# A hybrid decoder layer on one core: the first tokens' stage in an order written by hand, and the rope remainder product on 128 rows

## The chip, the core and the metric

The kernel runs on one core of one Trainium2 chip. A core has five engines that run their own instruction streams beside each other: TensorE (PE in the profile) multiplies matrices, VectorE (DVE), ScalarE (ACT) and GpSimd (POOL) work elementwise, and SyncE (SP) issues most transfers. Transfers run on 16 DMA engines. The metric is the device time of one execution in microseconds (us); the median of several runs is compared.

## The reference

One decoder layer on 512 tokens of width 1024, float32. A normalized input goes through one wide projection `w_in`; a gated linear recurrence (8 heads) and a latent attention (8 heads, causal) work on its columns; both are gated, projected and merged. The parts that the change touches are the first normalization and the scores of the attention:

```python
def rms_norm(x, g):
    y = xf * lax.rsqrt(jnp.mean(xf * xf, axis=-1, keepdims=True) + EPS)
    return (y * g.astype(jnp.float32)).astype(x.dtype)
...
h = rms_norm(x, norm_g[l])
proj = h @ w_in[l]
...
s = (jnp.einsum('bqhd,bkhd->bhqk', qn, k_nope)
     + jnp.einsum('bqhr,bkr->bhqk', qp, k_pe)).astype(jnp.float32) * scale
```

The rope part (`qp`, `k_pe`) has 64 numbers per head, the other part 128.

## The kernel before

**Precision.** A factor is held as two tiles of a shorter float type: a high part (a cast, on ScalarE) and a remainder (the factor minus its high part, on VectorE). A product of two such factors is three products on TensorE, high x high, high x low and low x high (`mm3`, lines 84 to 86). `load_w` fetches 512 KB of a weight into one of three buffers (`w_raw`), casts it (line 105) and subtracts (line 106); `split` does the same for a result in PSUM (lines 144, 145).

**First tokens' stage** (lines 168 to 227). x has four tiles of 128 tokens (t = 0 to 3). Twenty products on zeros (line 179) keep TensorE at work until x is there. x, the identity, the first projection's weights in two halves (`c_first`) and some small parameters are issued by SyncE; the norm weight `ng` is spread by a transfer over 128 partitions (line 190, 512 KB). For each tile: squares with a sum (ScalarE, line 213 or 216), the scale (for tile 0 on VectorE by an integer first guess and three Newton steps, lines 157 to 165; for the others on GpSimd by a power, lines 149 and 150), x times scale times `ng` (line 220, `xn`), eight transposes (line 225), and the split into `hT` (high part and remainder). The first projection, 256 columns from `COL_C`, is written behind that (`proj_tok`, line 271) and makes 24 products per tile of tokens; the next one of 256 columns follows.

**What sets the order.** The program is written without waits; a scheduler orders each engine's stream by a simulated time line, and an engine runs its stream strictly in that order. Transfers carry eight counters in turn (`DMAHW0` to `DMAHW7` in the orders below), and a transfer waits for the last one that used its counter. A weight buffer is free again when line 106 has read it.

**Scores** (`mla_scores`, lines 527 to 551). For a head, four blocks i of 128 queries against 128(i + 1) keys: three products of 128 rows over the part without rope (line 538, `mm3`, `kn` and `qn`), and two for rope. `qp[h % 2]` holds, in 128 rows, the high part of the rope query of this head in its own 64 rows and the remainder in the other 64; `kpe` holds the rope key twice, one copy per half, as high part `kpe[0]` and remainder `kpe[1]`. So one product on 128 rows with `kpe[0]` (line 539) gives high x high plus low x high, and one on the own 64 rows with `kpe[1]` gives high x low. That one is first in odd blocks (line 537) and last in even ones (line 541).

Of the kernel before, what the change touches and what calls it, by code (L numbers as in the profile page):

```python
# [40 lines left out]
def hybrid_layer(ctx: ExitStack, tc: tile.TileContext, a):  # L41
# [110 lines left out]
    def rsqrt_sum(rs, mul, add):  # L152


        v, y, c = [st.tile([P, 2], F32, f"rsq{i}") for i in range(3)]
        ts = nc.vector.tensor_scalar
        ts(v[:, 0:1], rs[:, 0:1], mul, add, op0=ALU.mult, op1=ALU.add)
        ts(v[:, 0:1], rs[:, 1:2], mul, v[:, 0:1], op0=ALU.mult, op1=ALU.add)
        ts(y[:, 0:1].bitcast(I32), v[:, 0:1].bitcast(I32), 1, None, op0=ALU.logical_shift_right)
        ts(y[:, 0:1].bitcast(I32), y[:, 0:1].bitcast(I32), -1.0, float(0x5F3759DF), op0=ALU.mult, op1=ALU.add)  # L160
        ts(v[:, 1:2], v[:, 0:1], -0.5, None, op0=ALU.mult)
        for i in range(3):
            ts(c[:, 0:1], y[:, 0:1], y[:, 0:1], v[:, 1:2], op0=ALU.mult, op1=ALU.mult)
            out = rs if i == 2 else y
            ts(out[:, 0:1], c[:, 0:1], 1.5, y[:, 0:1], op0=ALU.add, op1=ALU.mult)
# [41 lines left out]
    for t in range(NT):
        hs = [slice(n * 512, n * 512 + 512) for n in range(2)]
        sq = st.tile([P, D], F32, "sq", bufs=2)
        rs = st.tile([P, 2], F32, "rs", bufs=2)  # L210
        if t == 0:
            for n in range(2):
                nc.scalar.activation(sq[:, hs[n]], x_sb[t][:, hs[n]], AF.Square, accum_out=rs[:, n : n + 1])
            rsqrt_sum(rs, 1.0 / D, EPS)
        else:
            nc.scalar.activation(sq[:], x_sb[t][:], AF.Square, accum_out=rs[:, 0:1])
            power(rs[:, 0:1], rs[:, 0:1], 1.0 / D, EPS, neg_half[:, 0:1])
        xn = st.tile([P, D], F32, "xn", bufs=2)
        for n in range(2):
            nc.vector.scalar_tensor_tensor(xn[:, hs[n]], x_sb[t][:, hs[n]], rs[:, 0:1], ng[:, hs[n]], op0=ALU.mult, op1=ALU.mult)  # L220
# [528 lines left out]
```

## Time and profile before

| | |
|---|---|
| median of three runs | 653.09 us (653.09 to 654.28) |
| the profiled execution, in all | 653.86 us |
| its span, first to last instruction | 652.1 us |
| mean granted TensorE clock | 0.995 |
| bytes read from and written to memory | 55.53 MB, 2.10 MB |

The time in all is taken around the span. Rows of a time line give start and duration in us, engine and line, the operation, the written tile <- the tiles read, shape and count, and in brackets how long the engine idled before and what ended that. PE is a product, PEld the load of its stationary factor, ACTq and SPq the issue of a transfer. Products overlap, so the distance of two starts says what one costs. A wait row says who waited for whom, the total, how often, and the longest.

### The profile page before, as it was taken

The page shows a single profiled execution, that of the slowest core. Times are in us where ns is not written, and L with a number is a line of the kernel's source. Part 1 is how long each engine was busy: PE and PEld are TensorE (multiplying, and loading weights), DVE is VectorE, ACT ScalarE, POOL GpSimd, SP SyncE. Part 2 cuts the span into 40 slices and gives each one's busy share as a digit, 9 for nine tenths or more (in the row PEclk, how much of TensorE's full clock was granted, in tenths as well). Part 3 has the DMA queues.
Part 4 walks back from the last instruction along what each step waited for, and adds up shares of the span by engine and source line. Part 5 has one row for each costly group of instructions (what it writes and reads, how often), then busy time and mean ns, then how long its engine had stood idle before and what let it go on. Part 6 is the DMA issues. An engine that isn't in the chain of part 4 may idle for free.

```text
span 652.1 us, 9054 instructions
## 1 busy us (share of the span) xinstructions
PE 640.3 (98%) x3537; PEld 541.1 (83%) x3537; DVE 351.4 (54%) x546; ACT 239.1 (37%) x451; POOL 112.6 (17%) x211
## 2 busy tenths in 40 slices
PE   7999999999999999999999999999999999999995
PEld 3998988988998898888788888888888888888884
DVE  5725973784585397456665857745322342434244
ACT  6444333232333224254354545534222222323223
POOL 1105311320331232221213131000000010111011
PEclk9999999999999999999999999999999999999998
DMA  8343241233133014302323242133333323324403
GB/s 279 121 130 98 65 135 61 65 99 95 34 98 97 22 45 130 102 21 76 90 53 93 64 112 70 51 97 94 99 88 91 98 81 100 98 94 153 170 13 116
DMA packets 62023, 60.32 MB, mean 92 GB/s; under 512 B 5814, under 2 KB 57308, under 8 KB 61980
## 3 DMA queue, kind: packets, MB, share of 16 engines
q1 hardware_dynamic: 59628, 55.28, 28.5%
q10 hardware_dynamic: 2128, 3.67, 1.9%
q0 software_dynamic: 224, 0.79, 0.4%
q8 instruction: 28, 0.46, 0.3%
q14 instruction: 15, 0.12, 0.1%
HBM read 55.53 MB, written 2.10 MB: 88 GB/s over the span
## 4 chain that ended last, share of the span: by engine, by line
PE 97%; DMA 1%; DVE 1%; issue 0%; ACT 0%; SPq 0%; POOLq 0%; POOL 0%
PE mm_ps L86 26%; PE mm_ps L84 26%; PE mm_ps L85 26%; PE ax_ps L84 3%; PE ax_ps L85 2%; PE ax_ps L86 2%; PE ax_ps L562 1%; PE ax_ps L394 1%; PE ax_ps L413 1%; DMA w_raw<-w_in 1%; PE ax_ps L539 1%; PE ax_ps L415 1%; PE ax_ps L382 1%; PE ax_ps L541 1%; PE ax_ps L402 1%; PE ax_ps L537 1%
## 5 line engine op out<-in xcount | busy, mean ns | idle before, releaser
L106 DVE TENSOR_TENSOR w_lo<-w_raw,w_hi 128x1024 fp32r<-128x1024 f32 (+3 forms) x94 | 111.2, 1185 | 119.6 <-ACT w_hi L105 115.6
L105 ACT CAST w_hi<-w_raw 128x1024 fp32r<-128x1024 f32 (+3 forms) x94 | 92.0, 979 | 174.4 <-PE mm_ps L85 114.1
L84 PE MATMUL mm_ps<-hT,w_hi 128*128 128x512 f32 x384 | 151.4, 394 | 0.0
L86 PE MATMUL mm_ps<-hT,w_lo 128*128 128x512 f32 x384 | 150.4, 392 | 0.0
L85 PE MATMUL mm_ps<-hT,w_hi 128*128 128x512 f32 x384 | 149.9, 390 | 0.0
L86 PEld LDWEIGHTS mm_ps<-hT,w_lo 128*128 128x128 f32 x384 | 72.1, 188 | 14.9
L85 PEld LDWEIGHTS mm_ps<-hT,w_hi 128*128 128x128 f32 x384 | 72.2, 188 | 14.2
L84 PEld LDWEIGHTS mm_ps<-hT,w_hi 128*128 128x128 f32 x384 | 72.2, 188 | 14.2
L86 PE MATMUL mm_ps<-w_hi,hT 128*128 128x256 f32 (+1 forms) x224 | 63.6, 285 | 0.3 <-DVE hT L145 0.3
L84 PE MATMUL mm_ps<-w_hi,hT 128*128 128x256 f32 (+1 forms) x224 | 63.4, 283 | 0.0
L85 PE MATMUL mm_ps<-w_lo,hT 128*128 128x256 f32 (+1 forms) x224 | 63.3, 283 | 0.0
L86 PEld LDWEIGHTS mm_ps<-w_hi,hT 128*128 128x128 f32 x224 | 43.2, 193 | 0.8 <-DVE hT L145 0.7
L84 PEld LDWEIGHTS mm_ps<-w_hi,hT 128*128 128x128 f32 x224 | 43.3, 193 | 0.4 <-ACT hT L144 0.3
L85 PEld LDWEIGHTS mm_ps<-w_lo,hT 128*128 128x128 f32 x224 | 43.2, 193 | 0.2
L652 POOL TENSOR_TENSOR ma<-ma,z 128x512 f32<-128x512 f32 x8 | 11.8, 1478 | 163.9 <-DVE z L651 163.9
L549 POOL TENSOR_SCALAR p<-p,sm 128x128 f32<-128x128 f32 (+3 forms) x32 | 18.9, 597 | 116.1 <-DVE sm L548 89.7
L339 DVE RECIPROCAL tf<-pr 128x512 f32<-128x512 f32 x8 | 26.8, 3349 | 0.2
L547 ACT ACTIVATE p<-ax_ps,sm 128x128 f32<-128x128 f32 (+3 forms) x32 | 16.8, 528 | 25.3 <-DVE sm L546 20.8
L84 PE MATMUL mm_ps<-ya,w_hi 128*128 128x512 f32 x64 | 25.4, 396 | 0.0
L84 PE MATMUL mm_ps<-yb,w_hi 128*128 128x512 f32 x64 | 25.3, 396 | 0.0
L85 PE MATMUL mm_ps<-yb,w_hi 128*128 128x512 f32 x64 | 25.3, 396 | 0.0
L85 PE MATMUL mm_ps<-ya,w_hi 128*128 128x512 f32 x64 | 25.3, 396 | 0.0
(212 smaller groups left out, 1119.3 us busy)
## 6 DMA issues: line engine op xcount, KB each, us to landing
w_raw<-w_in SPq DMA_DIRECT2D x60, 512.0 KB, 3.8
w_raw<-w_proj_a SPq DMA_DIRECT2D x8, 512.0 KB, 3.4
w_raw<-w_proj_b SPq DMA_DIRECT2D x8, 512.0 KB, 3.4
wo_raw<-w_out SPq DMA_DIRECT2D x8, 512.0 KB, 3.3
w_raw<-w_ukv SPq DMA_DIRECT2D x16, 128.0 KB, 2.5
xr<-x SPq DMA_DIRECT2D x4, 512.0 KB, 7.3
x<-x SPq DMA_DIRECT2D x3, 512.0 KB, 8.0
w_raw<-w_uq SPq DMA_DIRECT2D x8, 192.0 KB, 2.6
```

The lines of the kernel that those rows point to most:

```text
L84: nc.tensor.matmul(ps, lh[lsl], rh[rsl], start=start, stop=False)
L85: nc.tensor.matmul(ps, lh[lsl], rl[rsl], start=False, stop=False)
L86: nc.tensor.matmul(ps, ll[lsl], rh[rsl], start=False, stop=stop)
L105: nc.scalar.copy(hi[:, :o], raw[:, :o])
L106: (lo_eng or nc.vector).tensor_tensor(lo[:, :o], raw[:, :o], hi[:, :o].bitcast(F32), op=ALU.subtract)
L339: nc.vector.reciprocal(rp[:], pr[:])
L382: nc.tensor.matmul(sps[:, sl], kt_[:, sl], v_sb[:, i, (h % 2) * P : (h % 2) * P + P], start=True, stop=True)
L394: nc.tensor.matmul(aps[:, b], ki[:, b], qi[:, b], start=True, stop=True)
L402: nc.tensor.matmul(aps[0:64, i * P + 64 : i * P + P], k64[:, b], q64[:, b], start=True, stop=True)
L547: nc.scalar.activation(p[:, :n], sps[:, :n], AF.Exp, scale=SCALE, bias=sm[:, 1:2], accum_out=sm[:, 2:3])
L549: nc.gpsimd.tensor_scalar(p[:, :n], p[:, :n], sm[:, 3:4], 0.5, op0=ALU.mult, op1=ALU.mult)
L652: nc.gpsimd.tensor_tensor(ma[:, j], ma[:, j], g[:], op=ALU.add)
```

## The change

It has two parts.

In the scores, the remainder product takes all 128 rows of `qp` and `kpe[1]` and always stands last. It then also holds the product of the two remainders, which was left out before. Both halves of `kpe[1]` were filled before too.

The first tokens' stage is written out for TensorE, ScalarE and VectorE in one block whose order the scheduler keeps among its own instructions (it may put others between). The norm weight comes as one row of 4 KB and is spread over the partitions by two products with a row of ones, into PSUM, where line 225 reads it. Tile 0's scale is a square root on ScalarE, a reciprocal and one Newton step. There are eight products on zeros in place of twenty. The first projection's weights are cast and split in pieces of 512 columns, the last piece's subtraction on GpSimd. Each tile's products with one kind of factor stand in groups of four. `ident` is issued by ScalarE, the rope table `ktab` by SyncE right ahead of the second projection's weights.

```diff
-    def rsqrt_sum(rs, mul, add):
...
-    nc.scalar.activation(warm[:], neg_half[:], AF.Tanh)
-    idle = ax_tile()
-    for i in range(N_IDLE):
-        nc.tensor.matmul(idle[:], zero[:, :P], zero[:], start=True, stop=True)
...
-    nc.scalar.dma_start(ng[:], a["norm_g"][0].partition_broadcast(P))
-    nc.sync.dma_start(ident[:], a["c_ident"])
-    c_first = [load_w(w_c0[:, 0:4, :])]
+    nc.scalar.dma_start(ng_row[:], a["norm_g"])
+    nc.scalar.dma_start(ident[:], a["c_ident"])
+    load_c(0)
     load_x(1)
-    c_first.append(load_w(w_c0[:, 4:8, :]))
+    load_c(1)
     load_x(2)
     load_x(3)
...
     nc.sync.dma_start(maskf[:], a["c_masks"])
+    nc.sync.dma_start(ktab[:], a["c_ktab"])
...
+    def c_split(kh, i, eng):
+
+        hi, lo = c_hl[kh]
+        nc.scalar.copy(hi[:, half[i]], c_raw[kh][:, half[i]])
+        eng.tensor_tensor(lo[:, half[i]], c_raw[kh][:, half[i]], hi[:, half[i]].bitcast(F32), op=ALU.subtract)
...
+    FIN = 1
+    with tc.manual_schedule(engines={mybir.EngineType.PE, mybir.EngineType.Activation, mybir.EngineType.DVE}):
+        nc.vector.memset(zero[:], 0.0)
+        nc.vector.memset(ones[:], 1.0)
+        nc.scalar.activation(warm[:], eps[:], AF.Sqrt)
+        idle_mm(5)
+        for n in range(2):
+            nc.tensor.matmul(ng[n][:], ones[:], ng_row[:, half[n]], start=True, stop=True)
+        idle_mm(3)
...
+        for n in range(2):
+            nc.scalar.activation(sq[:, half[n]], x_sb[0][:, half[n]], AF.Square, accum_out=rs[:, n : n + 1])
+        nc.vector.tensor_scalar(v[:], rs[:, 0:1], 1.0 / D, EPS, op0=ALU.mult, op1=ALU.add)
+        nc.scalar.activation(y[:], rs[:, 1:2], AF.Sqrt, scale=1.0 / D, bias=v[:])
+        nc.vector.tensor_scalar(e[:], rs[:, 1:2], 1.0 / D, v[:], op0=ALU.mult, op1=ALU.add)
+        nc.vector.tensor_scalar(e[:], e[:], -0.5, None, op0=ALU.mult)
+        nc.vector.reciprocal(y[:], y[:])
+        nc.vector.tensor_scalar(v[:], y[:], y[:], e[:], op0=ALU.mult, op1=ALU.mult)
+        nc.vector.tensor_scalar(rs[:, 0:1], v[:], 1.5, y[:], op0=ALU.add, op1=ALU.mult)
+        scaled(0)
+        c_split(0, 0, nc.vector)
+        lo0 = turned(0, 0)
+        lo0()
+        c_split(0, 1, nc.vector)
+        lo1 = turned(0, 1)
+        c_product(0, 0, 0)
+        c_product(0, 0, 1, (0, 1))
+        c_product(0, 0, 2)
+        c_product(0, 0, 1, (2, 3))
+        lo1()
+        squares(1)
+        c_split(1, 0, nc.vector)
+        c_split(1, 1, nc.gpsimd)
+        squares(2)
+        c_product(0, 1, 0)
+        c_product(0, 1, 2)
+        c_product(0, 1, 1)
+        scaled(1)
+        lo = [turned(1, 0), turned(1, 1)]
+        for t in range(1, NT):
+            if t + 2 < NT:
+                squares(t + 2)
+            for kh in range(2):
+                lo[kh]()
+            if t + 1 < NT:
+                scaled(t + 1)
+            for kind in (0, 1, 2):
+                c_product(t, 0, kind)
+            if t + 1 < NT:
+                nxt = [turned(t + 1, 0), turned(t + 1, 1)]
+            for kind in (0, 2, 1):
+                c_product(t, 1, kind)
+            lo = nxt
...
-        r = slice((h % 2) * 64, (h % 2) * 64 + 64)
...
-            if i % 2:
-                nc.tensor.matmul(sps[:, :n], qh[r, bl], kpe[1][r, :n], start=True, stop=False)
-            mm3(sps[:, :n], qn, kn, (slice(None), bl), (slice(None), slice(0, n)), i % 2 == 0, False)
-            nc.tensor.matmul(sps[:, :n], qh[:, bl], kpe[0][:, :n], start=False, stop=i % 2 == 1)
-            if i % 2 == 0:
-                nc.tensor.matmul(sps[:, :n], qh[r, bl], kpe[1][r, :n], start=False, stop=True)
+            mm3(sps[:, :n], qn, kn, (slice(None), bl), (slice(None), slice(0, n)), True, False)
+            for x in range(2):
+                nc.tensor.matmul(sps[:, :n], qh[:, bl], kpe[x][:, :n], start=False, stop=x == 1)
```

In the new block `scaled(t)` makes `xn`, `turned(t, k4)` transposes four of its columns' blocks and casts them (its result, called later, is the remainder's subtraction), `squares(t)` gives a tile's scale, and `c_product(t, kh, kind)` does four products of tile t with one half kh of the weight; kind 0 is high x high, 1 high x low, 2 low x high.

How the streams move, at the places that matter. First TensorE in the scores of head 0, blocks 0 and 1, before (`kpe_281` is the high part of the rope key, `kpe_282` its remainder):

```order
L84 MATMUL ax_ps<-kn_2616,qn_2605 128x128
L85 MATMUL ax_ps<-kn_2617,qn_2605 128x128
L86 MATMUL ax_ps<-kn_2616,qn_2606 128x128
L539 MATMUL ax_ps<-kpe_281,qp_2580 128x128
L541 MATMUL ax_ps<-kpe_282,qp_2580 128x128
L537 MATMUL ax_ps<-kpe_282,qp_2580 128x256
L84 MATMUL ax_ps<-kn_2616,qn_2605 128x256
L85 MATMUL ax_ps<-kn_2617,qn_2605 128x256
L86 MATMUL ax_ps<-kn_2616,qn_2606 128x256
L539 MATMUL ax_ps<-kpe_281,qp_2580 128x256
```

The same place after (`kpe_87` high part, `kpe_88` remainder):

```order
L82 MATMUL ax_ps<-kn_2615,qn_2604 128x128
L83 MATMUL ax_ps<-kn_2616,qn_2604 128x128
L84 MATMUL ax_ps<-kn_2615,qn_2605 128x128
L604 MATMUL ax_ps<-kpe_87,qp_2579 128x128
L604 MATMUL ax_ps<-kpe_88,qp_2579 128x128
L82 MATMUL ax_ps<-kn_2615,qn_2604 128x256
L83 MATMUL ax_ps<-kn_2616,qn_2604 128x256
L84 MATMUL ax_ps<-kn_2615,qn_2605 128x256
L604 MATMUL ax_ps<-kpe_87,qp_2579 128x256
L604 MATMUL ax_ps<-kpe_88,qp_2579 128x256
```

The count of products is the same; lines 541 and 537, on 64 rows and side by side across two blocks, have become the second of each pair of line 604, on 128 rows.

Second, ScalarE from the first weight cast to the casts of the second projection's weights, before. In brackets is what a row waits for; the waits of line 105 are for the weight's transfer:

```order
L105 CAST w_hi<-w_raw 128x1024 [waits DMAHW4_49]
L216 ACTIVATE sq,rs<-x 128x1024 [waits DMAHW5_49]
L105 CAST w_hi<-w_raw 128x1024 [waits DMAHW6_49]
L144 CAST hT_148<-ax_ps 128x4x128 [waits PE_49]
L216 ACTIVATE sq,rs<-x 128x1024 [waits DMAHW7_49,DVE_49,Activation_49]
L144 CAST hT_148<-ax_ps 128x4x128 [waits PE_49]
L216 ACTIVATE sq,rs<-x 128x1024 [waits DVE_49,DMAHW0_49,Activation_49,Pool_49]
L144 CAST hT_148<-ax_ps 128x4x128 [waits PE_49] x2
L105 CAST w_hi<-w_raw 128x1024 [waits DMAHW7_49]
L105 CAST w_hi<-w_raw 128x1024 [waits DMAHW0_49]
L144 CAST hT_148<-ax_ps 128x4x128 [waits PE_49] x4
```

And after, from the first weight cast on (line 215 casts the first projection's weights, line 103 the second's, line 235 the transposes):

```order
L215 CAST w_hi<-w_raw 128x512 [waits DMAHW4_49]
L235 CAST hT_112<-ax_ps 128x4x128 [waits PE_49]
L215 CAST w_hi<-w_raw 128x512
L235 CAST hT_112<-ax_ps 128x4x128 [waits PE_49]
L220 ACTIVATE sq,rs<-x 128x1024 [waits DMAHW5_49]
L215 CAST w_hi<-w_raw 128x512 [waits DMAHW6_49]
L215 CAST w_hi<-w_raw 128x512
L220 ACTIVATE sq,rs<-x 128x1024 [waits DMAHW7_49,DVE_49,Activation_49]
L103 CAST w_hi<-w_raw 128x1024 [waits DMAHW0_49]
L103 CAST w_hi<-w_raw 128x1024 [waits DMAHW1_49]
L235 CAST hT_112<-ax_ps 128x4x128 [waits PE_49] x2
```

Before, four casts of transposes (tiles 0 and 1) stand ahead of the two casts of the second projection's weights; after, two (tile 0) do, and tile 1's come behind them.

Third, SyncE's issues after x's third tile, after the change (line 179 is x's last tile, line 198 the rope table, line 100 the second projection's weights):

```order
L179 DMA x<-x 128x1024 [waits DMAHW0_49]
L192 DMA rows<-lb_logits 16x128 [waits DMAHW1_49]
L193 DMA rows<-b_gate 16x128 [waits DMAHW2_49]
L194 DMA rows<-hg_norm_g 1x128 [waits DMAHW3_49]
L195 DMA rows<-q_a_g 3x128 [waits DMAHW4_49]
L196 DMA rows<-kv_a_g 2x128 [waits DMAHW5_49]
L197 DMA maskf<-c_masks 128x256 [waits DMAHW6_49]
L198 DMA ktab<-c_ktab 128x512 [waits DMAHW7_49]
L100 DMA w_raw<-w_in 128x4x256 [waits DMAHW0_49]
L100 DMA w_raw<-w_in 128x4x256 [waits DMAHW1_49,DVE_49]
```

`DMAHW0` is x's last tile here, so the first of these weights is issued when x has landed whole. Before, the masks stood right ahead of the weights, the rope table was issued by GpSimd, and the first weight waited for `DMAHW7`, x's third tile.

More of the change, by code (lines that the diff above doesn't have):

```diff
@@ L12 @@
 U8 = mybir.dt.uint8
-I32 = mybir.dt.int32
 BF16 = mybir.dt.bfloat16
@@ L35 @@
 N_MM = 3
-N_IDLE = 20
 WCH = 1024
@@ L150, in power @@
         nc.gpsimd.tensor_tensor(out, out, expo, op=ALU.pow)
-    def rsqrt_sum(rs, mul, add):
[L155 to L165, printed above, removed]
+    cT = [cpool.tile([P, 5, S], F32R, f"cT{i}") for i in range(2)]
+    kpe = [cpool.tile([P, S], F32R, f"kpe{i}") for i in range(2)]
+    cw = Pool("cwork", "right")
+    ktab = cw.tile([P, NT, 2, NR], F32, "ktab")
+    c_sb = cw.tile([P, NT, 704], F32, "c_sb")
+    rows = cw.tile([38, P], F32, "rows")
+    maskf = cw.tile([P, 2, P], F32, "maskf")
     st = Pool("start", "right")
@@ new lines, in hybrid_layer, with idle_mm @@
+    nc.sync.dma_start(ktab[:], a["c_ktab"])
+    half = [slice(n * 512, n * 512 + 512) for n in range(2)]
+    rss = [st.tile([P, 2], F32, "rs", bufs=2) for _ in range(NT)]
+    xns = [st.tile([P, D], F32, "xn", bufs=2) for _ in range(NT)]
+    ng = [ax_tile() for _ in range(2)]
+    idle = ax_tile()
+    c_ps = [mm_tile() for _ in range(2)]
+    def idle_mm(n):
+        for _ in range(n):
+            nc.tensor.matmul(idle[:], zero[:, :P], zero[:], start=True, stop=True)
+    def c_split(kh, i, eng):
+        hi, lo = c_hl[kh]
+        nc.scalar.copy(hi[:, half[i]], c_raw[kh][:, half[i]])
+        eng.tensor_tensor(lo[:, half[i]], c_raw[kh][:, half[i]], hi[:, half[i]].bitcast(F32), op=ALU.subtract)
@@ new lines, in squares, with scaled, turned @@
+    def squares(t):
+        sq = st.tile([P, D], F32, "sq", bufs=2)
+        nc.scalar.activation(sq[:], x_sb[t][:], AF.Square, accum_out=rss[t][:, 0:1])
+        power(rss[t][:, 0:1], rss[t][:, 0:1], 1.0 / D, EPS, neg_half[:, 0:1])
+    def scaled(t):
+        for n in range(2):
+            nc.vector.scalar_tensor_tensor(xns[t][:, half[n]], x_sb[t][:, half[n]], rss[t][:, 0:1], ng[n][:],
+                                           op0=ALU.mult, op1=ALU.mult)
+    def turned(t, k4):
+        ps = ax_tile()
+        for k in range(4):
+            kk = 4 * k4 + k
+            nc.tensor.transpose(ps[:, k * P : k * P + P], xns[t][:, kk * P : kk * P + P], ident[:])
+        sl = (slice(None), slice(4 * k4, 4 * k4 + 4), slice(t * P, t * P + P))
+        nc.scalar.copy(hT[0][sl], ps[:].rearrange("p (k t) -> p k t", k=4))
+        return lambda: nc.vector.tensor_tensor(hT[1][sl], ps[:].rearrange("p (k t) -> p k t", k=4),
+                                               hT[0][sl].bitcast(F32), op=ALU.subtract)
@@ L230, in hybrid_layer @@
+    st.close()
     par = const.tile([P, 38], F32, name="par")
@@ L260, in hybrid_layer @@
     nc.vector.tensor_scalar(c2[:], lb[:], 0.5, 0.5, op0=ALU.mult, op1=ALU.add)
-    st.close()
-    cT = [cpool.tile([P, 5, S], F32R, f"cT{i}") for i in range(2)]
-    kpe = [cpool.tile([P, S], F32R, f"kpe{i}") for i in range(2)]
-    cw = Pool("cwork", "right")
-    ktab = cw.tile([P, NT, 2, NR], F32, "ktab")
-    nc.gpsimd.dma_start(ktab[:], a["c_ktab"])
-    c_sb = cw.tile([P, NT, 704], F32, "c_sb")
     for c0, w in ((0, 256), (256, 256), (512, 192)):
-        for t2, ps in enumerate(proj_tok(w_in, COL_C + c0, w, hT, None if c0 else c_first)):
+        for t2, ps in enumerate(proj_tok(w_in, COL_C + c0, w, hT) if c0 else c_ps):
             nc.scalar.copy(c_sb[:, 2 * t2 : 2 * t2 + 2, c0 : c0 + w],
```

50 lines of the change are left out of this document (22 added, 28 removed).

## The prediction

> **What bounds the kernel now.** I read the page first (busy shares and the chain that ended last), then who TensorE waited for, then the rows of the two places that the diff touches. The first lines are the page's busy row and chain; the third answers which wait of TensorE is the longest.
>
> ```profile
> PE 640.3 (98%) x3537; PEld 541.1 (83%) x3537; DVE 351.4 (54%) x546; ACT 239.1 (37%) x451; POOL 112.6 (17%) x211
> ...
> PE 97%; DMA 1%; DVE 1%; issue 0%; ACT 0%; SPq 0%; POOLq 0%; POOL 0%
> ...
> PE ax_ps L225 <- DVE xn L220: 3.3, 1, 3.3
> ```
>
> TensorE (PE) is the bound: 97% of the chain is its own work, and its only long wait is 3.3 us for the first normalized tile. So time is to be had in two ways: TensorE's real work starts earlier, or its products follow each other faster. The diff tries one of each. I count a product by the distance from its start to the next start, since busy times overlap.
>
> **The scores (rope remainder on 128 rows).** These are TensorE's products in order of time, with start, duration, line, tiles and shape: a 64-row product standing alone, then the first and the last pair of them.
>
> ```profile
> 321.53 0.34 PE L85 MATMUL ax_ps<-kn,qn 128*128 128x384 f32 x1
> 321.70 0.33 PE L86 MATMUL ax_ps<-kn,qn 128*128 128x384 f32 x1
> 321.96 0.49 PE L537 MATMUL ax_ps<-kpe,qp 64*128 64x512 f32 x1
> 322.39 0.50 PE L84 MATMUL ax_ps<-kn,qn 128*128 128x512 f32 x1
> 322.72 0.39 PE L85 MATMUL ax_ps<-kn,qn 128*128 128x512 f32 x1
> 322.95 0.40 PE L86 MATMUL ax_ps<-kn,qn 128*128 128x512 f32 x1
> ...
> 275.52 0.27 PE L86 MATMUL ax_ps<-kn,qn 128*128 128x128 f32 x1
> 275.63 0.27 PE L539 MATMUL ax_ps<-kpe,qp 128*128 128x128 f32 x1
> 275.83 0.32 PE L541 MATMUL ax_ps<-kpe,qp 64*128 64x128 f32 x1
> 276.00 0.33 PE L537 MATMUL ax_ps<-kpe,qp 64*128 64x256 f32 x1
> 276.25 0.39 PE L84 MATMUL ax_ps<-kn,qn 128*128 128x256 f32 x1
> 276.48 0.28 PE L85 MATMUL ax_ps<-kn,qn 128*128 128x256 f32 x1
> 276.60 0.28 PE L86 MATMUL ax_ps<-kn,qn 128*128 128x256 f32 x1
> ...
> 415.52 0.34 PE L539 MATMUL ax_ps<-kpe,qp 128*128 128x384 f32 x1
> 415.78 0.44 PE L541 MATMUL ax_ps<-kpe,qp 64*128 64x384 f32 x1
> 416.06 0.39 PE L537 MATMUL ax_ps<-kpe,qp 64*128 64x512 f32 x1
> 416.39 0.50 PE L84 MATMUL ax_ps<-kn,qn 128*128 128x512 f32 x1
> 416.73 0.40 PE L85 MATMUL ax_ps<-kn,qn 128*128 128x512 f32 x1
> 416.96 0.40 PE L86 MATMUL ax_ps<-kn,qn 128*128 128x512 f32 x1
> ```
>
> Among products of 128 rows a 384-wide one takes 0.17 (321.53 to 321.70), a 512-wide one 0.23 (322.72 to 322.95), a 256-wide one 0.12 (276.48 to 276.60), a 128-wide one 0.11 (275.52 to 275.63). Around the lone 64-row product, 321.70 to 322.72 is 1.02 for one 384-wide and two 512-wide: 0.17 + 0.23 + 0.23 = 0.63, so 0.39 too much. The first pair: 275.63 to 276.48 is 0.85 against 0.11 + 0.11 + 0.12 + 0.12 = 0.46, 0.39 too much. The last pair: 1.21 against 0.17 + 0.17 + 0.23 + 0.23 = 0.80, 0.41 too much. The excess is paid once per change of row count there and back, whether one or two products stand between. The 32 products of lines 537 and 541 form 24 such groups (16 alone, 8 pairs) in the rows from 275.8 to 416.7; read in the same way they exceed by 0.29 to 0.43 each, 8.8 us in sum. After the change these 32 products have the shape of line 539, which shows no excess between its neighbours, and none are added. So the edit takes up to **8.8 us** off the bounding engine. What could eat some of it is late input, since each head's softmax runs through VectorE, ScalarE and GpSimd between its scores and its transposes, and weights must be cast and split in time. No TensorE wait shows in this stretch, so I take 8.5, with 7.0 to 9.0 as bounds.
>
> The Trainium skill's "TensorE: Matmul & The Clock Gate", section "Packing small matmuls — row/col tiling", says that a weight load overlaps a running product only where the row groups differ; by that, 128 rows after 128 rows would not overlap, and widening would buy nothing. The rows disagree: 256-wide products follow each other every 0.12 us here, and the load between them alone has 0.19:
>
> ```profile
> L84 PEld LDWEIGHTS mm_ps<-w_hi,hT 128*128 128x128 f32 x224 | 43.3, 193 | 0.4 <-ACT hT L144 0.3
> ```
>
> **The first tokens' stage.** Before, in rows of TensorE, ScalarE and VectorE:
>
> ```profile
> 11.78 1.32 PE L225 MATMUL ax_ps<-ident,xn 128*128 128x128 f32 x8 [3.35 <-DVE xn L220]
> ...
> 17.12 0.28 PE L84 MATMUL mm_ps<-w_hi,hT 128*128 128x256 f32 x1
> 17.24 0.28 PE L85 MATMUL mm_ps<-w_lo,hT 128*128 128x256 f32 x1
> ...
> 9.75 1.06 ACT L216 ACTIVATE sq<-x 128x1024 f32<-128x1024 f32 x1 [0.19 <-DMA x<-x]
> ...
> 11.07 1.05 ACT L105 CAST w_hi<-w_raw 128x1024 fp32r<-128x1024 f32 x1 [0.18 <-DMA w_raw<-w_in]
> ...
> 15.53 1.07 ACT L144 CAST hT<-ax_ps 128x512 fp32r<-128x512 f32 x2
> ...
> 18.65 1.05 ACT L105 CAST w_hi<-w_raw 128x1024 fp32r<-128x1024 f32 x1 [1.10 <-DMA w_raw<-w_in]
> ...
> 13.63 1.22 DVE L106 TENSOR_TENSOR w_lo<-w_raw,w_hi 128x1024 fp32r<-128x1024 f32 x1
> 14.77 0.68 DVE L145 TENSOR_TENSOR hT<-ax_ps,hT 128x512 fp32r<-128x512 f32 x1
> ...
> 18.16 1.40 DVE L220 SCALAR_TENSOR_TENSOR xn<-x,rs,ng 128x512 f32<-128x512 f32 x2
> ```
>
> By 17.12 TensorE has started 16 transposes (0.11 each) and 9 products (0.12): 2.8 us of work. From there it runs without a gap, so it stands where a TensorE would that began at 17.1 - 2.8 = 14.3 and never paused. The same number is needed for the change.
>
> Tile 0 gets faster: the 512 KB of the spread norm weight no longer travel beside x, the subtraction of 1.2 us no longer stands ahead of its scale, and three Newton steps become one. But the order of ScalarE shows what then decides: both casts of the *second* projection's weights stand ahead of the casts of tile 1's transposes, and they wait for their transfers. Call W the landing of the second of these (18.6 before, where ScalarE idles 1.10 for it). Then: its cast ends at W + 1.05, tile 1's first cast at W + 1.65 (first products of tile 1), the second at W + 2.15. VectorE's subtraction for that weight, also queued ahead, ends at W + 2.3, tile 1's two remainders at W + 2.9 and W + 3.5, tile 2 scaled (1.40) at W + 4.9, its last transposes issued at W + 5.45 and 12 products later W + 6.85. By then 48 products and 24 transposes are done, 8.35 us, so the equivalent start is W - 1.5. Against 14.3 that is **W - 15.8**.
>
> Rows for W (SyncE's issues of the two transfers, and the page's row on how long such a one takes):
>
> ```profile
> 12.38 0.40 SPq L102 DMA_DIRECT2D w_raw<-w_in  x1
> 13.78 0.38 SPq L102 DMA_DIRECT2D w_raw<-w_in  x1
> ...
> w_raw<-w_in SPq DMA_DIRECT2D x60, 512.0 KB, 3.8
> ```
>
> The second was issued at 13.78 and landed by 18.65: 4.9. After the change the first waits for x's last tile and the second is issued some 0.4 behind it. In the rows above, x and weights land in steps of 1.3 us per 512 KB (9.75, 11.07), which puts x's last tile at 13.7 before. Without the norm weight it comes at least one step earlier (12.4), and at most three, as the slow start beside that transfer goes too (9.8). I take two (11.1), and 4.5 for the transfer, nearer to the 4.9 because two run together again: W = 11.1 + 0.4 + 4.5 = 16.0; from the ends, 9.8 + 0.4 + 3.8 = 14.0 and 12.4 + 0.4 + 4.9 = 17.7. So the stage comes to +0.2 us, between -1.8 and +1.9: **what tile 0 gains is spent waiting ahead of tile 1.**
>
> All else in the stage is covered by that wait. Tile 0's first transposes stood at 11.78; without the subtraction (1.22) and with x one step earlier (1.3) they come by 9.3 at the latest. Then follow 16 transposes and 24 products, 4.6 us, and some 2 us of waits for ScalarE, which does a Square (1.06) and a cast (1.05) between: tile 1's transposes end by 15.9, ahead of W + 1.65 = 17.65. That hides the square root, the weight-spreading products, GpSimd's half subtraction (512 wide; its nearest row is the 1.48 of line 652) and the second table load. If W falls below 13, that cover is gone, and GpSimd's 1.5 us stands on the path.
>
> **Sum:** -8.5 + 0.2 = -8.3. The profiled execution had 653.9 in all, so 645.6; it lay 0.8 above the median of 653.1, so the median after should be **644.8 us**.
>
> **The rivals.**
>
> 1. *The start gains in full* (18%): the two transfers land early enough that tile 1 waits for nothing. Tile 0's transposes would begin by my estimate at 7.5 (9.3 less a further step of the transfers and half a us of Newton steps); with 2.6 us of waits in tile 0 (ScalarE, GpSimd) and 1.2 for tile 2's scale, the equivalent start is 11.3, 3 us better than 14.3: 653.1 - 8.5 - 3.0 = 641.6. Against: SyncE's queue issues these transfers behind x's last tile.
>
> 2. *The scores are held by their inputs* (8%): half the gain turns into waits for ScalarE and VectorE: 653.1 - 4.3 + 0.2 = 649.0. Against: VectorE is busy 54%, and TensorE waits for nobody there.
>
> 3. *The clock stays low* (7%). The windows (length, busy times, then granted clock) show half clock after the wait of 3.35 us:
>
> ```profile
> 14.00:16.00 2.00, 1.68 (x8) 1.27 (x7) 2.00 (x5) 2.00 (x7) 1.63 (x3) 0.50 0.89 266
> 18.00:20.00 2.00, 2.00 (x20) 2.00 (x19) 2.00 (x4) 1.26 (x2) 0.00 (x0) 1.00 0.43 145
> ```
>
> The change has 12 fewer warming products and, by my times, a wait of about 3 us ahead of tile 1. A product at half clock costs 0.21, not 0.12; 40 of them are 3.6 us: 644.8 + 3.6 = 648.4. For: waits as long as the old one. Against: work on tile 1 would run slow while VectorE holds it up anyway. The Trainium skill ("TensorE: Matmul & The Clock Gate", "Why this matters for your kernels") asks for no gaps above about 3 us, which the old wait bears out.
>
> 4. *The excess isn't of the row count* (5%), but of reading kpe's remainder tile, so it stays: 653.1 + 0.2 = 653.3, no change. Against: line 539 changes that tile too and pays nothing.
>
> 5. *ScalarE's queue jams, slower* (2%): each us that W comes later costs one, since ScalarE can't pass the cast. It is even at W = 15.8 + 8.5 = 24.3 and slower by 0.2% at 25.6; at 26 it gives 654.8. For: SyncE waited once 5.1 us for VectorE to free a weight buffer. Against: W is 18.6 even before.
>
> ```profile
> SPq L102 <- DVE w_lo L106: 6.4, 3, 5.1
> ```
>
> **Chances.** The forecast has 60%; the rest as given. A measurement of this kernel tells about 0.2% (1.3 us) from no change: faster 0.93 (forecast and rivals 1 to 3), same 0.05, slower 0.02. The forecast's own bounds are 653.1 - 9.0 - 1.8 = 642.3 and 653.1 - 7.0 + 1.9 = 648.0; taking in rival 1 below and part of 3 above, 641.0 to 648.8.
>
> **What would show it.** No 64-row rows in the scores and steps of 0.11 to 0.23 throughout: right on the large term; steps of 0.3 and more that remain: wrong. In the start, ScalarE idle ahead of the second weight cast on a transfer, with tile 1's casts right behind and TensorE waiting for them: right on the small one; tile 1's products before 15 us: rival 1. A granted clock of 0.50 after 20 us: rival 3. New TensorE waits between 270 and 410 us: rival 2.

## The result, and the profile after

The changed kernel takes **648.6 us** (median of four runs, 648.01 to 648.94) against 653.68 for the kernel before on the same chip (four runs): a ratio of 0.992, with a 95% interval of 0.9903 to 0.9937. It is 0.8% faster, 3.8 us above the time that was given and just inside the range of 641.0 to 648.8. The profiled execution of after took 648.64 us in all, its span 646.9.

The page's busy row and chain, and TensorE's waits, of the changed kernel:

```profile
PE 633.7 (98%) x3529; PEld 541.4 (84%) x3529; DVE 350.9 (54%) x543; ACT 240.7 (37%) x455; POOL 113.8 (18%) x212
...
PE 96%; DMA 2%; SPq 0%; issue 0%; ACT 0%; DVE 0%; POOLq 0%; POOL 0%
```

```profile
PE mm_ps L244 <- ACT hT L235: 3.3, 1, 3.3
PE mm_ps L244 <- DVE w_lo L216: 1.2, 1, 1.2
...
PE mm_ps L244 <- ACT w_hi L215: 0.6, 1, 0.6
```

The old wait of 3.3 us for tile 0's scale is gone. In its place stand 0.6 and 1.2 inside tile 0, and a new 3.3 ahead of tile 1's products (line 244), for ScalarE's cast of tile 1's transposes (line 235).

Two places of TensorE's stream say where the time went. The first product with `kpe` started at 275.63 before and starts at 278.86 now, so the start **lost 3.23 us**. The last product of the kernel's stream started at 644.73 and starts at 639.56 now, 5.17 earlier, so the rest **gained 8.40**.

In the scores every distance is now that of 128 rows (TensorE in order of time; the remainder product stands second in each pair of line 604):

```profile
279.25 0.28 PE L83 MATMUL ax_ps<-kn,qn 128*128 128x256 f32 x1
279.37 0.28 PE L84 MATMUL ax_ps<-kn,qn 128*128 128x256 f32 x1
279.49 0.41 PE L604 MATMUL ax_ps<-kpe,qp 128*128 128x256 f32 x2
279.73 0.34 PE L82 MATMUL ax_ps<-kn,qn 128*128 128x384 f32 x1
```

From 279.49 to 279.73 two products of 256 columns take 0.24, that is 0.12 each. The same reading over all groups with `kpe` finds an excess of 0.2 us in sum, where it was 8.8.

The start, in rows of SyncE, ScalarE, VectorE and TensorE:

```profile
12.06 0.35 SPq L198 DMA_DIRECT2D ktab<-c_ktab  x1
13.32 0.38 SPq L100 DMA_DIRECT2D w_raw<-w_in  x1
...
17.60 1.04 ACT L103 CAST w_hi<-w_raw 128x1024 fp32r<-128x1024 f32 x1 [3.41 <-DMA w_raw<-w_in]
19.10 1.04 ACT L103 CAST w_hi<-w_raw 128x1024 fp32r<-128x1024 f32 x1 [0.46 <-DMA w_raw<-w_in]
20.05 1.06 ACT L235 CAST hT<-ax_ps 128x512 fp32r<-128x512 f32 x2
...
13.96 0.63 DVE L317 COPY mask_inf<-maskf 128x128 f32<-128x128 f32 x1 [1.97 <-DMA maskf<-c_masks]
...
15.25 1.39 DVE L225 SCALAR_TENSOR_TENSOR xn<-x,rs,ax_ps 128x512 f32<-128x512 f32 x2
...
16.13 1.29 PE L233 MATMUL ax_ps<-ident,xn 128*128 128x128 f32 x8
20.68 1.22 PE L244 MATMUL mm_ps<-w_hi,hT 128*128 128x256 f32 x4 [3.26 <-ACT hT L235]
...
23.41 1.29 PE L233 MATMUL ax_ps<-ident,xn 128*128 128x128 f32 x8
24.45 1.19 PE L244 MATMUL mm_ps<-w_hi,hT 128*128 128x256 f32 x8
...
25.96 0.64 PE L244 MATMUL mm_ps<-w_hi,hT 128*128 128x256 f32 x4
```

(23.41 are tile 2's transposes, 24.45 is the second half of tile 1's products, 25.96 the first of tile 2's.)

Tile 1's transposes are done at 17.4, but ScalarE can't cast them: it stands idle for 3.41 and 0.46 us at the casts of the second projection's weights (line 103), which its stream has first. The chain of waits names the two transfers behind that:

```profile
3.79 9.52 DMA x<-x
...
13.82 5.26 DMA w_raw<-w_in
19.08 0.02 issue
```

x's last tile landed at 3.79 + 9.52 = 13.31 (13.69 before), the second weight half at 13.82 + 5.26 = **19.08**. That is the W of the prediction, and W - 15.8 = 3.28 against the 3.23 that the start lost. Between W and the scores the steps came as forecast, too: tile 1's products start at W + 1.60 (forecast W + 1.65), tile 2's at W + 6.88 (W + 6.85). The formula held; W had been put at 16.0. Once it had risen (at 10.24 us), the granted clock was half in one stretch of the start, behind the new wait (length, busy times, then clock, DMA share and GB/s):

```profile
17.05:20.48 3.43, 0.37 (x4) 0.13 (x2) 1.53 (x2) 2.42 (x3) 0.00 (x0) 1.00 0.68 217
20.48:23.89 3.41, 3.21 (x15) 3.15 (x16) 3.41 (x5) 1.68 (x4) 1.56 (x5) 0.50 0.69 159
23.89:27.30 3.41, 3.41 (x31) 3.40 (x30) 2.41 (x5) 1.66 (x3) 0.73 (x3) 1.00 0.34 115
```

### The profile page after: what moved, and what is told of

Same layout as the page of the kernel before. It is cut to its first block, busy times and chain, and to the rows that moved or that the text cites. A ratio compares the mean times of both kernels' runs of the same rounds, so it can differ in the third digit from the quotient of the medians.

```text
span 646.9 us, 9040 instructions
## 1 busy us (share of the span) xinstructions
PE 633.7 (98%) x3529; PEld 541.4 (84%) x3529; DVE 350.9 (54%) x543; ACT 240.7 (37%) x455; POOL 113.8 (18%) x212
## 4 chain that ended last, share of the span: by engine, by line
PE 96%; DMA 2%; SPq 0%; issue 0%; ACT 0%; DVE 0%; POOLq 0%; POOL 0%
PE mm_ps L82 26%; PE mm_ps L84 26%; PE mm_ps L83 26%; PE ax_ps L82 2%; PE ax_ps L83 2%; PE ax_ps L84 2%; PE ax_ps L604 2%; PE mm_ps L244 2%; DMA x<-x 1%; PE ax_ps L625 1%; PE ax_ps L461 1%; PE ax_ps L480 1%; PE ax_ps L482 1%; PE ax_ps L449 1%; DMA w_raw<-w_in 1%; PE ax_ps L469 1%
## 5 line engine op out<-in xcount | busy, mean ns | idle before, releaser
L103 ACT CAST w_hi<-w_raw 128x1024 fp32r<-128x1024 f32 (+3 forms) x92 | 89.8, 976 | 167.7 <-PE mm_ps L83 108.1
L84 PE MATMUL mm_ps<-w_hi,hT 128*128 128x256 f32 (+1 forms) x192 | 54.3, 283 | 0.0
L82 PE MATMUL mm_ps<-w_hi,hT 128*128 128x256 f32 (+1 forms) x192 | 54.2, 282 | 0.0
L83 PE MATMUL mm_ps<-w_lo,hT 128*128 128x256 f32 (+1 forms) x192 | 54.1, 282 | 0.0
L612 POOL TENSOR_SCALAR p<-p,sm 128x128 f32<-128x128 f32 (+3 forms) x32 | 20.3, 638 | 105.1 <-DVE sm L611 65.7
L82 PEld LDWEIGHTS mm_ps<-w_hi,hT 128*128 128x128 f32 x192 | 36.6, 191 | 0.2
L83 PEld LDWEIGHTS mm_ps<-w_lo,hT 128*128 128x128 f32 x192 | 36.6, 190 | 0.2
L84 PEld LDWEIGHTS mm_ps<-w_hi,hT 128*128 128x128 f32 x192 | 36.6, 190 | 0.0
L84 PE MATMUL mm_ps<-ya,w_lo 128*128 128x512 f32 x64 | 25.3, 395 | 0.0
L83 PE MATMUL mm_ps<-yb,w_hi 128*128 128x512 f32 x64 | 25.2, 394 | 0.0
```

The source lines that it names most:

```text
L82: nc.tensor.matmul(ps, lh[lsl], rh[rsl], start=start, stop=False)
L83: nc.tensor.matmul(ps, lh[lsl], rl[rsl], start=False, stop=False)
L84: nc.tensor.matmul(ps, ll[lsl], rh[rsl], start=False, stop=stop)
L103: nc.scalar.copy(hi[:, :o], raw[:, :o])
L612: nc.gpsimd.tensor_scalar(p[:, :n], p[:, :n], sm[:, 3:4], 0.5, op0=ALU.mult, op1=ALU.mult)
```

## The experiments

**The two parts alone.** The theory: the start costs 3.2 us of what the scores give, and the parts don't touch each other. First the kernel before with the new `mla_scores` only:

```diff
-            if i % 2:
-                nc.tensor.matmul(sps[:, :n], qh[r, bl], kpe[1][r, :n], start=True, stop=False)
...
+            for x in range(2):
+                nc.tensor.matmul(sps[:, :n], qh[:, bl], kpe[x][:, :n], start=False, stop=x == 1)
```

> The kernel before with the change of the scores alone. Theory (the start costs 3.2 us of what the scores give; the two do not touch each other): the whole excess at 24 changes of row count goes, 8.4 us by the traces, so 653.7 - 8.4 = 645.3, with TensorE's first products of the scores starting where they start before (275.6) and steps of 0.11 to 0.23 in the scores. Rival (the start is even, the scores are partly held by their inputs and give about 5): 648.6, and new waits of TensorE between 275 and 415 us.

Measured: 645.3 against 653.3, ratio 0.9876 (0.9862 to 0.9889). From the first to the last product with `kpe` the trace counts 133.05 us, where the kernel before has 141.57: 8.52 less. No wait of TensorE came up in the scores. (They start at 276.24, 0.6 later than before. The half clock of the start lasted up to 17.90 in this execution, in place of 17.05, which may be why.)

Then the changed kernel with the old `mla_scores`:

> The changed kernel with the scores as before, so the start alone. Theory: the start is slower by 3.2 us, 653.7 + 3.2 = 656.9, and the first product of the scores starts at about 278.9 where before it starts at 275.6. Rival (the start is even and the loss is elsewhere): 653.7. The sum of the two parts is to give the whole: with the scores alone at 645.3, this one has to come out at 656.9 for a whole of 648.6.

Measured: 657.28 against 653.3, ratio 1.0058 (1.0046 to 1.0071). The scores start at 278.79 and last 141.59, as before the change. So the start alone is **slower than the kernel before**, and the whole gain of the change, and more, is the scores'. The medians give -8.0 and +4.0 for the parts and -5.1 for the whole; each is known to 0.8 to 1.1 us, and the places in the traces (-8.5, +3.2, -5.2) add up.

**What in the scores costs.** Only line 541 of the kernel before widened, the even blocks:

```diff
-                nc.tensor.matmul(sps[:, :n], qh[r, bl], kpe[1][r, :n], start=False, stop=True)
+                nc.tensor.matmul(sps[:, :n], qh[:, bl], kpe[1][:, :n], start=False, stop=True)
```

> The kernel before with the remainder product widened to 128 rows in the even blocks alone (line 541). The 8 pairs of 64-row products become 8 single ones, the 16 single ones become: 8 that stay (odd blocks), 8 that go. Theory (the excess of 0.39 us is paid once per change of row count there and back): 16 groups of 64-row products stay, each a single one, and the 8 that vanish give 8 x 0.37 = 3.0 us: 653.5 - 3.0 = 650.5 (bounds 650.0 to 651.0). Rival (the excess belongs to each 64-row product, and one in a pair costs half of one alone): 16 of 32 products go with half of the 8.8 us, 649.1, or more precisely the groups that stay with one product would show 0.2 of excess where they were pairs.

Measured: 651.45 against 653.66, ratio 0.9968 (0.9956 to 0.998). That is 2.2 us (by the interval 1.3 to 2.9), outside the bounds of the theory, though nearer to it than to the rival. The trace decides. A former pair that is now a single product (TensorE in order of time, this kernel):

```profile
276.70 0.34 PE L539 MATMUL ax_ps<-kpe,qp 128*128 128x384 f32 x1
276.87 0.34 PE L541 MATMUL ax_ps<-kpe,qp 128*128 128x384 f32 x1
277.14 0.49 PE L537 MATMUL ax_ps<-kpe,qp 64*128 64x512 f32 x1
277.56 0.50 PE L84 MATMUL ax_ps<-kn,qn 128*128 128x512 f32 x1
277.90 0.39 PE L85 MATMUL ax_ps<-kn,qn 128*128 128x512 f32 x1
```

From 276.87 to 277.90 is 1.03 for a 384-wide and two 512-wide, 0.63 by their own distances: 0.40 too much with one 64-row product, as it was with two. All eight former pairs still exceed by 0.38 to 0.40, the 16 groups by 6.15 in sum. So the excess belongs to the change of row count, and a second 64-row product beside the first is free. The theory's 3.0 was too high because the eight singles that went cost 8.77 - 6.15 = 2.62 together, 0.33 each, less than the mean of all groups. The Trainium skill says in "TensorEngine Tiling (Array Packing)", section "Tiling Modes", that changing the tiling mode drains TensorE; these rows agree, and put 0.3 to 0.4 us on a change there and back.

**What decides the start.** The load, the casts and the subtractions of the second projection's weights go into the hand-written block, behind the scaling of tile 3; nothing is added or taken away:

```diff
             if t + 1 < NT:
                 scaled(t + 1)
+            if t == 2:
+                c_second = load_cols(w_in, COL_C + 256)
```

> The changed kernel with the load, the casts and the subtractions of the second projection's weights placed behind the scaling of tile 3 in the hand-written order; no work is added or taken away. ScalarE then casts the transposes of tiles 1 and 2 before it waits for those weights. Theory (the wait for the landing of the second weight half, 19.05 us, decides the start, because ScalarE's stream has the cast for it ahead of tile 1): tile 1's products start at about 17.4 in place of 20.7 us, the granted clock stays at 1.0 between 20 and 24 us, and the time falls by 3.7 us to 644.9 (bounds 644.3 to 645.7). Rival (the late transfers themselves or the half clock decide; the casts' place is only where the wait is seen): no gain over 0.6 us, 648.0 to 648.6.

Measured: 644.8 against 653.3, ratio 0.9865 (0.9852 to 0.9879), so 3.8 below the changed kernel. ScalarE and TensorE of this kernel:

```profile
16.80 1.24 ACT L235 CAST hT<-ax_ps 128x512 fp32r<-128x512 f32 x2 [2.61 <-PE ax_ps L233]
...
20.23 1.25 ACT L235 CAST hT<-ax_ps 128x512 fp32r<-128x512 f32 x2 [1.14 <-PE ax_ps L233]
21.38 2.00 ACT L103 CAST w_hi<-w_raw 128x1024 fp32r<-128x1024 f32 x2
...
17.44 0.74 PE L244 MATMUL mm_ps<-w_hi,hT 128*128 128x256 f32 x4
```

ScalarE now casts tile 1 at 16.80 in place of 20.05, and tile 1's products start at 17.44 in place of 20.68. When it comes to the weights at 21.38 they are there. The scores start at 275.02, 0.6 ahead of the kernel before.

**Whether the half clock costs.** Twelve more products on zeros behind tile 1's transposes keep TensorE at work in the wait:

```diff
         lo = [turned(1, 0), turned(1, 1)]
+        idle_mm(12)
```

> The changed kernel with twelve more products on zeros behind tile 1's transposes, so that TensorE has work during its wait of 3.3 us ahead of tile 1's products. Theory (VectorE holds the path behind the wait, so the half clock costs nothing): the clock is granted in full between 20.5 and 23.9 us, the time stays at 648.6, plus or minus 0.5. Rival (the half clock costs what 12 products at 0.22 in place of 0.12 us give): 1.2 us less, 647.4.

Measured: 648.66, ratio 0.9928 (0.9914 to 0.9941). The clock was full, the time the same, as this window of the kernel shows:

```profile
20.48:23.89 3.41, 2.37 (x16) 1.97 (x16) 3.41 (x5) 1.76 (x4) 1.48 (x5) 1.00 0.62 155
```

VectorE's 3.41 (third of the busy times, the whole stretch) fits the reason given: TensorE waits for it there at any clock.

**The next wait.** To the moved casts comes the move of VectorE's two mask copies (lines 317, 318 of the changed kernel, which the scheduler had put ahead of tile 1's scale) to the end of the block:

```diff
             lo = nxt
+        nc.vector.tensor_copy(mask_inf[:], maskf[:, 1])
+        nc.vector.tensor_copy(mask_le[:], maskf[:, 0])
```

> The changed kernel with the casts of the second projection's weights behind tile 2's (as in the run on that) and, in addition, VectorE's two copies of the mask moved from their place ahead of tile 1's scale to the end of the hand-written block. Theory (behind the first wait stands a second one: VectorE waits 2.06 us for the mask's transfer, up to 14.05, and tile 1's scale and the last weight remainder of tile 0 stand behind it): tile 1's products start at 16.0 where they start at 17.44 with the casts moved alone, and the time falls by 1.4 us to 643.4 (bounds 643.0 to 644.0). Rival (GpSimd's half subtraction, which ends at 14.5, and tile 1's landing hold tile 0's last products as long anyway): under 0.5 us, 644.3 to 644.8.

Measured: 643.52, ratio 0.9846 (0.9833 to 0.986), 1.3 below the moved casts alone. VectorE's row of tile 1's scale in this kernel, 13.27 in place of 15.25:

```profile
13.27 1.40 DVE L225 SCALAR_TENSOR_TENSOR xn<-x,rs,ax_ps 128x512 f32<-128x512 f32 x2
```

**Whether tile 0 is covered.** The three products on zeros ahead of tile 0's transposes are taken out, once of the changed kernel (there, and in two runs below, with the second projection's load and the mask's copies written into the block where they stood, so that no order changes with the edit), once of the version just told:

```diff
-        idle_mm(3)
```

> The changed kernel, its order on ScalarE and VectorE kept by hand, without the three products on zeros that stand between the spreading of the norm weight and tile 0's transposes. They keep TensorE busy up to 8.4 us, while the second half of tile 0 is scaled at 8.0 and the first at 7.3. Theory (all of tile 0's stage is covered by the wait for the second weight half, so what tile 0 gains is lost ahead of tile 1): tile 0's transposes start at 7.3 in place of 8.4, the first product of the scores stays at 278.9, and the time at 648.6, plus or minus 0.5. Rival (tile 0 is on the path): 1.1 less, 647.5.

> The same three products on zeros taken out of the version that has the casts of the second projection's weights behind tile 2's and the masks at the end. There the wait is gone, and the cover with it. Theory: tile 0's start is now on the path, transposes at 7.3 in place of 8.4, and the time falls by 0.8 to 1.1, to 642.4 to 642.7 from 643.5. Rival (x's and the weights' landings at 9.3 and 10.7 hold the rest of tile 0 and tile 1's scale anyway): 643.5, no change.

Measured: 649.32 (ratio 0.9937, 0.9925 to 0.995) for the changed kernel without them, 642.71 (0.9837, 0.9823 to 0.985) for the other, **the lowest time of this study**. In the first, tile 0's transposes start 0.6 earlier (7.76) and nothing is gained; it even lost 0.7, a little outside the bounds, of which more below. In the second, where no wait covers tile 0, the same edit gives 0.8: the scores start at 272.95, and at 273.74 with the products on zeros. (The intervals of the two ratios overlap; the traces carry this one.)

**Why W came late.** Three runs on the transfers. In the first, ScalarE issues the first projection's two weight halves, so that two queues run side by side; in the next the same is added to the version with the two moves:

```diff
-        nc.sync.dma_start(c_raw[kh][:].rearrange("p (k c) -> p k c", k=4), w_c0[:, 4 * kh : 4 * kh + 4, :])
+        nc.scalar.dma_start(c_raw[kh][:].rearrange("p (k c) -> p k c", k=4), w_c0[:, 4 * kh : 4 * kh + 4, :])
```

> The changed kernel with the two transfers of the first projection's weights issued by ScalarE (behind the identity's) and not by SyncE between x's tiles; all else as it is, ScalarE's casts of the second projection's weights ahead of tile 1's too. Theory (between 3.5 and 5 us the one queue of x and weights doesn't fill the DMA engines, which move 50 to 80 KB per half us there and 190 later; two queues side by side do): x's last tile lands at 12.0 in place of 13.3, the second weight half at about 17.7 in place of 19.05, and the time falls by just as much, 1.3 us, to 647.3 (bounds 646.5 to 648.0). That would also show a second time that the stage is the landing of that half less 15.8. Rival (the transfers are held by single slow packets and DMA engines, not by the queue): x's last tile at 13.0 or later, 648.3 to 648.9.

> The changed kernel with the casts of the second projection's weights moved behind tile 2's, the mask's copies at the end of the block, and the first projection's weights issued by ScalarE. Theory: as with the first two moves alone, 643.4, less what earlier weights give to tile 0, whose products wait 0.6 and 1.2 us for casts and remainders of the weights that land at 8.0 and 10.8: 642.4 (bounds 641.8 to 643.4). Rival (x's first tiles now share the DMA engines with the weights, tile 0's scale comes later by as much): 643.4 to 644.4.

Measured: 648.82 (ratio 0.9926, 0.9913 to 0.9938) and 647.22 (0.9903, 0.989 to 0.9917). Both theories failed, and where the first time is the rival's, it isn't for the rival's reason. x's last tile landed at about 11. From 4 to 6 us the DMA engines moved 348 GB/s in the first run and 256 in the other (235 in the changed kernel, which moved 94 to 110 KB per half us from 3.5 to 5 us, not the 50 to 80 that the expectation gives). But the first weight half then landed at 10.9 and 11.8 (7.98 without the edit), since it shares the engines with all of x. In the first run that made tile 0 late, so that VectorE freed the weight buffer only at 13.5, and the second half of the second projection was issued behind that: W fell just 0.4, to 18.65. In the other run tile 0 itself is the path, and 3.7 us were lost. How much of that is the later weights and how much the clock isn't separated: in that run eight products of tile 0 still take 1.71 (15.82 to 17.53), 0.21 each, and the clock rose at 19.31 only.

The next puts the old 512 KB transfer back, into a tile that nobody reads:

```diff
     nc.scalar.dma_start(ng_row[:], a["norm_g"])
+    nc.scalar.dma_start(spread[:], a["norm_g"][0].partition_broadcast(P))
```

> The changed kernel, its order on ScalarE and VectorE kept by hand, with the 512 KB transfer of the kernel before (the norm weight spread over 128 partitions, issued by ScalarE) added again, into a tile that nobody reads. Theory (that transfer ran in time in which one queue doesn't fill the DMA engines, so it cost x's last tile next to nothing, and taking it away gave next to nothing): x's last tile lands 0.3 to 0.6 later than 13.3, the second weight half as much later than 19.05, and the time is 648.9 to 649.2. Rival (the prediction's reading: 512 KB are a step of 1.3 us, and the slow start beside them a second one): x's last tile at 14.6 or later, 649.9 to 651.2.

Measured: 650.64 (ratio 0.9955, 0.9943 to 0.9968). The theory fell and the rival held. The chain of waits of this run:

```profile
4.18 10.52 DMA x<-x
```

x's last tile landed at 14.70, 1.39 later than in the changed kernel. Of the 2.0 us that this run takes longer, W accounts for 1.2 and the clock for most of the rest (the table below). Yet taking the 512 KB away had moved that landing from 13.69 to 13.31 only, so something else must have taken most of the step away from the changed kernel. The last run changes the order on the one queue: x's second tile ahead of the first weight half.

```diff
-    load_c(0)
     load_x(1)
-    load_c(1)
+    load_c(0)
     load_x(2)
+    load_c(1)
```

> The changed kernel, its order on ScalarE and VectorE kept by hand, with x's second tile issued ahead of the first half of the first projection's weights (and x's third ahead of the second half); the same transfers on the same queue. In the runs so far the first weight half, issued second, moves only 24 to 80 KB per half us from 3.5 to 5 us while nothing else stands in its place, and x's tiles behind it land 1.3 us apart. Theory (a weight half with its 512 pieces of 1 KB starts flowing later after its issue than a tile of x with its 128 pieces of 4 KB, and the engines stand partly empty for that; with x's tile in between they don't): the engines move over 100 KB per half us throughout from 2 to 5 us, x's last tile lands at 12.3 to 12.7 in place of 13.3, the second weight half 0.6 to 1.0 earlier than 19.05, and the first product of the scores starts that much earlier than 278.9: 647.6 to 648.0 in all. Rival (the start of any second transfer is slow, or single engines lag whatever is queued): x's last tile at 13.2 or later and 648.6, plus or minus 0.4.

Measured: 649.09 (ratio 0.9933, 0.9919 to 0.9947). The window from 4 to 6 us (the last two numbers are the DMA share and GB/s) is in the kernel before:

```profile
4.00:6.00 2.00, 2.00 (x6) 0.76 (x5) 0.00 (x0) 0.12 (x1) 0.00 (x0) 1.00 0.96 291
```

in the changed kernel:

```profile
4.00:6.00 2.00, 2.00 (x3) 0.66 (x2) 0.61 (x4) 1.25 (x5) 0.00 (x0) 1.00 0.85 235
```

and in this run:

```profile
4.00:6.00 2.00, 2.00 (x3) 0.67 (x2) 0.18 (x2) 0.84 (x5) 0.00 (x0) 1.00 0.88 302
```

Its rows of SyncE and ScalarE:

```profile
12.49 0.93 SPq L100 DMA_DIRECT2D w_raw<-w_in  x2
...
18.28 1.04 ACT L103 CAST w_hi<-w_raw 128x1024 fp32r<-128x1024 f32 x1 [0.46 <-DMA w_raw<-w_in]
```

SyncE issues the next weights at 12.49, as soon as x's last tile is there, 0.83 earlier than in the changed kernel, and W is 18.25, also 0.83 earlier. That is what the theory said of the landings, but it doesn't show the reason. Seven versions issue these transfers in the changed kernel's order (that kernel, the start alone, the moved casts, the warm wait, the moved masks, and the two without three products on zeros). From 4 to 6 us they moved 181 to 345 GB/s, and SyncE issued the next weights, that is, x's last tile was there, at 12.75 to 13.95. The version with the moved masks even moved more than this run:

```profile
4.00:6.00 2.00, 2.00 (x3) 0.66 (x2) 0.75 (x5) 1.45 (x5) 0.00 (x0) 1.00 1.02 345
```

So one execution at 302 and 12.49 is a hint that the order matters, no more. Nor does the rate from 4 to 6 us set the landing: the warm wait, at 181, issued the next weights at 13.31, the changed kernel, at 235, at 13.32. And the time didn't fall. The scores start at 279.31, where W - 15.8 puts them at 275.63 + 2.45 = 278.08. The windows of the run, cut where the clock changes, show what took the rest:

```profile
18.96:22.37 3.41, 2.51 (x12) 2.51 (x12) 3.12 (x6) 2.38 (x5) 0.86 (x3) 0.50 0.56 127
22.37:25.79 3.42, 3.42 (x17) 3.36 (x17) 2.03 (x5) 1.17 (x2) 1.43 (x5) 0.50 0.46 147
25.79:29.20 3.41, 3.41 (x31) 3.41 (x30) 1.39 (x3) 0.59 (x1) 0.00 (x0) 1.00 0.00 0
```

Tile 2's transposes and the second half of tile 1's products fall into the second of these stretches:

```profile
22.58 1.94 PE L233 MATMUL ax_ps<-ident,xn 128*128 128x128 f32 x8
24.17 1.92 PE L244 MATMUL mm_ps<-w_hi,hT 128*128 128x256 f32 x8
25.92 0.64 PE L244 MATMUL mm_ps<-w_lo,hT 128*128 128x256 f32 x4
26.40 0.64 PE L244 MATMUL mm_ps<-w_hi,hT 128*128 128x256 f32 x4
```

The eight transposes take 1.59 to the next start (1.04 in the changed kernel), the eight products 1.75 (1.03), and tile 2's products start at 26.40, which is W + 8.15 in place of W + 6.88. In all runs that keep ScalarE's order (times in us; before, the scores start at 275.63):

| run | W | W - 15.8 | start of the scores, later by | half clock behind tile 1's wait |
|---|---|---|---|---|
| the change | 19.08 | 3.28 | 3.23 | to 23.89 |
| start alone | 18.88 | 3.08 | 3.16 | to 23.96 |
| warm wait | 19.15 | 3.35 | 3.30 | none |
| two queues | 18.65 | 2.85 | 2.80 | none |
| three idle products fewer | 19.52 | 3.72 | 4.49 | 22.60 to 26.01 |
| 512 KB more | 20.29 | 4.49 | 5.24 | 23.37 to 26.78 |
| x's tile first | 18.25 | 2.45 | 3.68 | 18.96 to 25.79 |

Where the clock is full when the second half of tile 1's products starts (5.4 to 5.9 us behind W), the formula holds to 0.1 us. Where it isn't, 0.75 to 1.2 us come on top. The three runs with an excess are also those whose order was kept by hand, but ScalarE, VectorE and GpSimd run the changed kernel's instructions in its order in this stage, and in all seven runs tile 1's products start at W + 1.6 and tile 2's transposes at W + 4.3. The excess arises behind that, where the products are slow.

## Why the prediction was right, and where it was off

The large term was right, in size and for its reason, and it makes the change faster; the small one, put at +0.2, came to +3.2. Of the 3.8 us that the time lies above the forecast, 3.0 are the start's, and 0.6 come of the kernel before, which took 653.68 beside the change in place of 653.1. That the measured 648.6 lies inside the range is luck: the forecast's own bounds end at 648.0, and the range had been widened to 648.8 for rival 3, which cost nothing here.

- **Scores, -8.5 (bounds -9.0 to -7.0):** right in mechanism and size. The trace gives 8.40 in the changed kernel and 8.52 with the scores alone. The reading "once per change of row count there and back" is shown by the widened even blocks. Rivals 2 (held by inputs) and 4 (excess not of the row count) fall.
- **Start, the formula W - 15.8:** right. It held in four runs to 0.1 us, its steps came where they were put, and moving the casts that it is about took 3.8 us away.
- **Start, W = 16.0:** this is the step that failed: a term that was mis-sized. W was 19.08. Of the 3.1 us, 2.2 are the landing of x's last tile (put at 11.1 after "two steps", measured 13.31), 0.76 the transfer behind it (put at 4.5, measured 5.26, above its upper bound of 4.9) and 0.1 the issue. Neither of the two steps came. The first, 1.3 us for 512 KB, fits the run that adds them again (1.39), yet taking them away brought 0.4 (13.69 to 13.31; x's last tile landed between 13.6 and 14.0 in the three versions with the old start, and between 12.7 and 14.0 in the seven versions that issue the transfers as the changed kernel does). The second, "as the slow start beside that transfer goes too", fell: the kernel before moved 291 GB/s from 4 to 6 us and the changed one 235, so the slow start stayed. Why is open; a queue with x's second tile ahead of the first weight half landed x's last tile at 12.49, beside the 12.4 of the prediction's own upper end, in one execution. That `ktab` (256 KB) now stands right ahead of the second projection's weights was named in the description of the change but left out of W. It may be why that transfer took 5.05 to 5.34 in all seven runs of the table, where it took 4.85 before; no run took it away, so that stays open.
- **"All else in the stage is covered":** right. Tile 0 gained 0.6 without any gain in time; with the wait gone the same edit gave 0.8. But the cover was thinner than it was put: tile 1's transposes ended at 17.42, not by 15.9, so at the W of 16.0 they would have been just ahead of W + 1.65. What the prediction hadn't seen is a second wait behind the first: VectorE's mask copy, 1.97 idle for its transfer, worth 1.3 us once the casts were moved.
- **Rival 3, the clock:** half clock came after 20 us as it said, and cost nothing in the changed kernel, for the reason held against it (VectorE holds that stretch). But the cover is thin: three other versions paid 0.75 to 1.2 for it.
- **Rival 1 (the start gains in full, 641.6):** it didn't happen. With both waits moved away the start gains 275.63 - 273.74 = 1.9, and with three products on zeros fewer 275.63 - 272.95 = 2.7, near the 3.0 that the rival put on it: most of it was there, and the order of the change gave it back.

## What to carry to other kernels

When a stage gets faster, look in each engine's stream for what stands ahead of the next stage's work and waits for a transfer: here two casts for a later projection cost more than the whole stage had gained, and moving them behind was worth 3.8 us. Price a landing with its spread and not by bytes alone: 512 KB fewer brought 0.4 us where two steps of 1.3 had been expected, and the same transfers in the same order were there up to 1.2 us apart. A few products on fewer rows among products on all rows cost by the change, so widen them or put them side by side.

## What the runs showed of the hardware

- **A change of TensorE's row count** (128 to 64 and back) costs 0.3 to 0.4 us whether one or two products stand between.
- **The granted clock moves in steps of 3.41 us** that don't begin with the program. It rose at 10.24 us in the profiled execution of the change, at 12.36 without the three products on zeros and at 12.13 with x's tile first, and each fall to half in a start lasted 3.41 or 6.83. The Trainium skill says so in "TensorE: Matmul & The Clock Gate", section "What's actually happening": a free-running window of 3413 ns that isn't reset when a kernel starts. The runs agree. It makes what a wait costs depend on where the steps fall, as the table shows.
- **The same transfers don't land at the same time.** With the same transfers in the same order at the start, seven versions moved 181 to 345 GB/s from 4 to 6 us, one profiled execution each, and x's last tile was there at 12.75 to 13.95. In the changed kernel four single packets of 4 KB took 0.8 to 1.3 us in that stretch, where most take 0.16. What causes either is open.
